# Hybrid attention layer: the rotary chain traced with the second pair of forgetting heads, x's parts added on VectorE, two steps a tile, other banks for the first latent keys

## The chip, the cores and the metric

The kernel runs on one core of one Trainium2 chip. The core has a matrix engine (TensorE, in the profile PE, with its weight loads as PEld), VectorE (DVE), ScalarE (ACT), GpSimd (POOL), SyncE (SP), which here only issues transfers, and 16 DMA engines. On-chip memory is SBUF, and PSUM, eight banks of 128 x 512 numbers into which PE writes. The metric is device time in microseconds, median of the runs shown. Lower is better.

## The reference

The layer takes x (512 tokens, 2048 wide, float32), normalizes it and projects it with one wide matrix. The columns are the latents and gate of eight latent-attention heads (MLA), and queries, keys, values, forget logits and gate of eight forgetting heads (FoX). Both attend causally, both are gated, and one output projection follows.

```python
h = _rms_norm(x, g_pre)
proj = h @ w_in
(q_lat, kv_lat, k_rope_raw, gate_mla,
 fq, fk, fv, f_logit, gate_fox) = jnp.split(proj, split_points, axis=-1)
o_mla = _mla_branch(q_lat, kv_lat, k_rope_raw, g_q, w_uq, g_kv, w_ukv, cos, sin) * jax.nn.silu(gate_mla)
o_fox = _fox_branch(fq, fk, fv, f_logit, b_forget) * jax.nn.silu(gate_fox)
o = jnp.concatenate([o_mla, o_fox], axis=-1) @ w_out
return x + _rms_norm(o, g_post)
```

In the MLA branch the latents are normalized and projected up to queries, keys and values; 64 of the 192 query and key numbers of a head are turned by the rotary tables, the sine and cosine of position times frequency. In the FoX branch the logits get the running sum of the log of a sigmoid of the forget logits (the scan below).

## The kernel before, in words

**Numbers.** Products run at nearly full float32 precision from rounded parts. Each operand is divided into a high part (a copy rounded on ScalarE, line 290 for weights) and a low part (the rest, subtracted on VectorE, line 291), and PE adds three products (lines 152 to 154). A weight tile is 128 x 1024 numbers. `chunk` (line 291 is in its helper `divide`) loads tiles four ahead and divides them two ahead; the pools whi and wlo hold three tiles each.

**Products.** Large projections (values "v" and gate "g" of the forgetting heads, latents and MLA gate, the values' up projection, the output) run as seven block products instead of eight, p1, p2, g5, g3, g7, q6, p4, on sums and differences of blocks. This needs differences of the blocks of x: `x_steps(j)` for j = 0 to 3 puts four pairs of x's high and low parts together again (tile xr, line 1117), then `away_steps` subtracts blocks (tile rmg, line 1016), keeps one difference divided (smg), and sends the others to DRAM through POOL's queue (awaymg, line 1006), to be fetched later on SyncE (bmg, line 1045). Tiles of x parts, copied values and the first scaled query share one pool of four, differences and many weight tiles a pool of 28 slots.

**Stages.** First x is transposed, and a part of the projection (with the forget logits) runs to 42 us. Then come the first forgetting queries (`fox_q(0, ...)`, tile fq), with the forget sums (`forget_sums`: powers, logs, ends, rows, scan) beside it; then p1 of the values (tile va) and of the gate (ga), p2, and the other products. Four pairs of forgetting heads follow (`for p in range(4)`): in round p the queries of pair p are projected while the scores of the pair before run, and the keys while that pair's probabilities meet the values. Then the latent products, four pairs of MLA heads (`mla_q`, `mla_k`, `mla_values`), and the output.

**Order.** Work beside the matmuls stands in a list, `todo`. After each k tile of a product `pump(rate)` takes that many steps off the list and traces them; `wait(n)` puts in n empty steps; `drain()` traces all that is left. The order in which the code traces instructions is their priority. A planner then sets each engine's order, ahead of the run: from the instructions whose inputs it expects to be ready, it takes the one traced first. So an instruction that is ready early may stand far ahead of its place in the code. On the chip each engine, and each of the DMA queues of SyncE and POOL, works in that order, and what waits holds up all behind it. `queued()` ties a load on SyncE behind the weight load traced last. In the first projection the orders of PE, ScalarE and VectorE are as written.

**Rotary tables.** `rotary_tables` (traced after product g3 of the gate) issues five small loads on SyncE (lines 874 and 876: frequencies and positions), then steps: one cast and eight other scalings on VectorE and sixteen steps of subtracting turns or the like (lines 883 to 918, tile angles), three sines on ScalarE (lines 917 to 920), one write to DRAM on POOL (line 921), eight loads on SyncE that spread the tables (line 926). The tables are first used by the rotary key, after the forgetting heads.

**Banks.** PSUM's eight banks are four for projections (`proj_bank`), three for attention (`att_bank`) and one more ("pv"). `mla_q(0)` takes three projection banks, from which small copies (tile mw, line 126) and other work read; the first keys `mla_k(0, ...)` follow a product uA, which has one projection bank and "pv".

Of the kernel before, what the change touches and what calls it, by code (L numbers as in the profile page):

```python
# [65 lines left out]
def tile_hybrid_layer(  # L66
# [36 lines left out]
    def bank(tag, name, bufs):  # L103
        return ps.tile([P, 512], F32, tag=tag, name=name, bufs=bufs)

    def proj_bank(name):
        return bank("pj", name, 4)

    def att_bank(name):
        return bank("at", name, 3)  # L110
# [481 lines left out]
    def wait(n):  # L592
        todo.extend([lambda: None] * n)
# [19 lines left out]
    def proj_T(rng, outs, kh, kl, rate=1, ahead_load=4):  # L613

        k = 0
        n_k = sum(chunks[i][3] for i in rng)
        for i in rng:
            hi, lo = chunk(i, ahead_load)
            for j in range(chunks[i][3]):
                for o, rows, pick in outs:  # L620
                    mm3(o[:rows, :], pick(hi, j), pick(lo, j), kh[k], kl[k], k == 0, k == n_k - 1)
                k += 1
                pump(rate)
                paced(hi)
# [244 lines left out]
    def rotary_tables():  # L869
        ifc = cst.tile([P, 2], F32, name="ifc")  # L870
        rows = cst.tile([P, 3, P], F32, name="angles")
        r, n1, n2 = (rows[:, i, :] for i in range(3))
        with queued():
            nc.sync.dma_start(ifc, inv_freq)
            for b in range(NT):
                nc.sync.dma_start(
                    r[32 * b : 32 * (b + 1), :].bitcast(I32),
                    positions[:, b * P : (b + 1) * P].to_broadcast([32, P]),
                )
        steps = []  # L880

        def angles():
            dve.tensor_copy(n1, r.bitcast(I32))
            dve.tensor_scalar(out=r, in0=n1, scalar1=ifc[:, 0:1], scalar2=None, op0=ALU.mult)

        steps.append(angles)

        def turns(n, c):
            def step():
                dve.tensor_scalar(out=n, in0=r, scalar1=1.0 / c, scalar2=RND, op0=ALU.mult, op1=ALU.add)  # L890
                dve.tensor_scalar(out=n, in0=n, scalar1=-RND, scalar2=None, op0=ALU.add)

            steps.append(step)

        def take(n, parts):
            for c in parts:
                steps.append(
                    lambda c=c: dve.scalar_tensor_tensor(
                        out=r, in0=n, scalar=-c, in1=r, op0=ALU.mult, op1=ALU.add
                    )  # L900
                )

        turns(n1, 2 * math.pi * 4096)
        take(n1, BIG_TURN[:4])
        turns(n2, 2 * math.pi)
        take(n2, TURN[:3])
        take(n1, BIG_TURN[4:])
        take(n2, TURN[3:])
        turns(n1, 2 * math.pi)
        take(n1, TURN[:4])  # L910
        to = dr.tile([P, 3 * P], F32, name="tables")

        def sines():
            lim = 3.1415925
            dve.tensor_scalar(out=r, in0=r, scalar1=lim, scalar2=-lim, op0=ALU.min, op1=ALU.max)

            act.activation(n2, r, AF.Sin, scale=-1.0)
            dve.scalar_tensor_tensor(out=n1, in0=r, scalar=-1.0, in1=r, op0=ALU.mult, op1=ALU.max)
            act.activation(r, r, AF.Sin)
            act.activation(n1, n1, AF.Sin, scale=-1.0, bias=half)  # L920
            pool.dma_start(to, rows.rearrange("p n c -> p (n c)"))

        def spread():
            for g in range(4):
                for table, n in ((sinT, 2 * (g % 2)), (cosT, 1)):
                    nc.sync.dma_start(
                        table[32 * g : 32 * (g + 1), :].rearrange("f (b c) -> f b c", b=NT),
                        to[:, n * P : (n + 1) * P].rearrange("(b f) c -> f b c", b=NT),
                    )

        return [*steps, sines, spread]
# [177 lines left out]
    def x_steps(j):  # L1109

        pair = []

        def whole(h, i):
            if not pair:
                pair.extend(v_block(f"xr{n}{j}") for n in range(2))
            k = 2 * j + 8 * h + i
            pool.tensor_tensor(out=pair[h][:, i, :], in0=hh[k].bitcast(F32), in1=hl[k].bitcast(F32), op=ALU.add)
            if h and i:
                todo.extendleft(reversed(away_steps("m", j, pair, keep="g5")))

        return [lambda h=h, i=i: whole(h, i) for h in range(2) for i in range(2)]
# [1 line left out]

    o_of = []

    def fox_q(p, qb, place):

        proj_T(fox[p]["q"], [(qb[i], P, two[i]) for i in range(2)], hh, hl)
        both = place(f"fqr{p}")
        for i in range(2):  # L1130
            dve.scalar_tensor_tensor(
                out=both[:, i, :], in0=qb[i], scalar=SC_F, in1=rrow, op0=ALU.mult, op1=ALU.mult
            )
        return both

    def fox_q_parts(p, both):

        wholes = slot(f"fw{p}")
        q = []
        for i in range(2):  # L1140
            q.append(split(both[:, i, :], f"fq{p}{i}", first=P))
            whole_block(wholes, i, both[:, i, :])
        return q, wholes
# [92 lines left out]
    def gate_step(h):  # L1236

        g = gate_slots[h // 2][:, h % 2, :]
        gate_of(g, g, f"f{h}")
# [12 lines left out]
    def two_of(make, name):  # L1252
        return [make(f"{name}{i}") for i in range(2)]
# [10 lines left out]
    pool.dma_start(l4_away, l4.rearrange("p t c -> p (t c)"))  # L1264
    dg = diagonals(rcol, "rrow")
    fs = forget_sums(rft)
    wait(2)
    todo.append(lambda: make_row(rrow, "rrow", *dg))
    set_pace(1000)
    todo.extend(fs[:3])  # L1270
    wait(1)
    todo.extend([*x_steps(0), *fs[3:], *x_steps(1)])
    places = [(g, j) for g in "vg" for j in range(4)]
    for g, j in places[:5]:
        fill(prods["p1", g][j], vr.tile([P, 1024], F32, tag="raw", name=f"raw{g}{j}", bufs=5))
    q0 = fox_q(0, [att_bank("fq00"), bank("pv", "fq01", 1)], v_block)
    for g, j in places[5:]:
        fill(prods["p1", g][j], wp.tile([P, 1024], F32, tag="raw", name=f"raw{g}{j}", bufs=3))
    drain()
# [98 lines left out]
    for g in "vg":  # L1378
# [4 lines left out]
    products(  # L1383
        "vg", ("g5", "g3", "g7", "q6", "p4"),
        {
            ("g5", "v"): (1, d3), ("g5", "g"): (1, f7), ("g3", "g", "after"): lambda: todo.extend(rotary_tables()),
            ("g3", "v"): (1, d7), ("g3", "g"): (1, f6), ("g7", "v"): (1, d6),
        },
        out_of,
# [16 lines left out]
    for p in range(4):  # L1406
        if p:
            todo.extend(lambda h=h: gate_step(h) for h in (6 - 2 * p, 7 - 2 * p))
            q, wholes = fox_q_parts(p, fox_q(p, two_of(proj_bank, f"fq{p}"), slot))
            drain()  # L1410
            keys = [load_keys(2 * (3 - p) + i, wholes) for i in range(2)]
            vt = load_v(3 - p, v_slot(3 - p))
            enqueue_values(heads)
            todo.insert(10, split_v(3 - p, vt))
            k = fox_k(p, wholes)
            keys = [forget_keys(*a) for a in keys]
            drain()
        else:
            keys = [forget_keys(*a) for a in keys]
            vt = v_slot(3)  # L1420
            later = split_v(3, vt)
        if p == 2:
            with queued():
                nc.sync.dma_start(gains[0:6, :], g_q.rearrange("o (k p) -> (o k) p", p=P))
                nc.sync.dma_start(gains[6:10, :], g_kv.rearrange("o (k p) -> (o k) p", p=P))
            make_gcol(gains, NK, 10)
        vs = values_of(f"fv{3 - p}")
        heads = []
        for i in range(2):
            h = 2 * (3 - p) + i  # L1430
            heads.append(
                Head(
                    f"f{h}", [q[i]], [k[i]],
                    vs[i],
                    lambda h=h: gate_slots[h // 2][:, h % 2, :],
                    [tuple(wholes[:, 0, c * P : (c + 1) * P] for c in (i, 2 + i))], keys[i],
                )
            )
        enqueue_scores(heads, 1)
        if p == 0:  # L1440
            todo.insert(12, lambda vt=vt: load_v(3, vt))
            todo.append(later)
# [7 lines left out]
    def raw(i):  # L1450
        return raws_of[(i // 2 + 1) % 5][:, i % 2, :]
# [15 lines left out]
    def latent_stats(j):  # L1467
        for s in stats_steps(j):
            s()
# [115 lines left out]
    beside.clear()  # L1585
    room.close()
    todo.extend(lambda i=i: latent(i, raw(i)) for i in range(4))
    todo.append(lambda: latent_stats(0))

    def gate_later(h):  # L1590
# [53 lines left out]

    def mla_k(p, wholes):

        kb = [proj_bank(f"mk{p}{i}") for i in range(2)]
        proj_T(mla[p]["k"], [(kb[i], P, two[i]) for i in range(2)], *k_parts, 2, 6)
        kw = [[whole_block(wholes, 2 + i, kb[i]), krw] for i in range(2)]
        return [[split(kb[i], f"mk{p}{i}"), tuple(keys_turned)] for i in range(2)], kw  # L1650
# [283 lines left out]
```

## Time and profile before

| | us |
|---|---|
| median of 3 runs | 905.74 (904.56 to 906.33) |
| profiled execution | 907.51 |
| its span, first to last instruction | 905.7 |
| PE busy | 879.7 |
| VectorE busy | 633.0 |
| ScalarE busy | 499.9 |
| POOL busy | 145.9 |
| PE's mean granted clock | 0.989 of full speed |

The profile is of one execution. Its page gives busy times, the span in 40 slices and the costliest groups; other views group instructions by tile or line, list who waited for whom, and give busy time by stage. Tiles stand as output<-inputs, without buffer numbers. Matmuls overlap, so that their single durations add up to more than PE's time.

### The profile page before, as it was taken

The page shows a single profiled execution, that of the slowest core. Times are in us where ns is not written, and L with a number is a line of the kernel's source. Part 1 is how long each engine was busy: PE and PEld are TensorE (multiplying, and loading weights), DVE is VectorE, ACT ScalarE, POOL GpSimd, SP SyncE. Part 2 cuts the span into 40 slices and gives each one's busy share as a digit, 9 for nine tenths or more (in the row PEclk, how much of TensorE's full clock was granted, in tenths as well). Part 3 has the DMA queues.
Part 4 walks back from the last instruction along what each step waited for, and adds up shares of the span by engine and source line. Part 5 has one row for each costly group of instructions (what it writes and reads, how often), then busy time and mean ns, then how long its engine had stood idle before and what let it go on. Part 6 is the DMA issues. An engine that isn't in the chain of part 4 may idle for free.

```text
span 905.7 us, 13772 instructions
## 1 busy us (share of the span) xinstructions
PE 879.7 (97%) x5078; PEld 775.1 (86%) x5078; DVE 633.0 (70%) x1043; ACT 499.9 (55%) x914; POOL 145.9 (16%) x148
## 2 busy tenths in 40 slices
PE   8995899999999999999999999999999999999996
PEld 8984799999988888888999999977788888887885
DVE  4669856658555454646677678789787886988786
ACT  6932454435336354544755445547766877646383
POOL 2136402442110100100004442200000000000021
PEclk9997999999999999999999999999999999999999
DMA  9486978999669788794689999985959645799878
GB/s 287 121 282 185 285 229 198 220 229 230 156 147 219 189 228 241 189 264 123 198 294 253 247 223 239 229 217 125 233 141 237 176 132 185 241 321 307 277 216 249
DMA packets 128488, 198.41 MB, mean 219 GB/s; under 512 B 16338, under 2 KB 61292, under 8 KB 127396
## 3 DMA queue, kind: packets, MB, share of 16 engines
q1 hardware_dynamic: 101428, 136.28, 48.2%
q0 software_dynamic: 26256, 61.02, 34.3%
q8 instruction: 40, 0.66, 0.3%
q10 hardware_dynamic: 736, 0.22, 0.1%
q14 instruction: 28, 0.23, 0.1%
HBM read 182.60 MB, written 44.25 MB: 250 GB/s over the span
## 4 chain that ended last, share of the span: by engine, by line
PE 78%; DVE 9%; DMA 6%; ACT 3%; issue 2%; SPq 1%; DVEq 0%; ACTq 0%
PE fk L152 3%; PE fk L154 3%; PE fk L153 3%; DVE wlo L291 3%; PE fq L152 2%; PE fq L154 2%; PE fq L153 2%; PE sm L698 2%; PE in L655 2%; PE sf L698 2%; PE oa L154 2%; PE oa L153 2%; PE oa L152 2%; PE mq L154 1%; PE mq L153 1%
## 5 line engine op out<-in xcount | busy, mean ns | idle before, releaser
L291 DVE TENSOR_TENSOR wlo<-raw,whi 128x1024 fp32r<-128x1024 f32 (+3 forms) x159 | 186.7, 1177 | 108.7 <-ACT whi L290 106.1
L290 ACT CAST whi<-raw 128x1024 fp32r<-128x1024 f32 (+3 forms) x159 | 160.4, 1012 | 142.7 <-PE fk L153 35.5
L152 PE MATMUL fk<-h,whi 128*128 128x512 f32 x128 | 52.5, 410 | 0.0
L152 PE MATMUL fq<-h,whi 128*128 128x512 f32 x128 | 50.9, 397 | 0.0
L154 PE MATMUL fk<-h,wlo 128*128 128x512 f32 x128 | 50.3, 393 | 0.0
L153 PE MATMUL fk<-h,whi 128*128 128x512 f32 x128 | 50.0, 391 | 0.0
L154 PE MATMUL fq<-h,wlo 128*128 128x512 f32 x128 | 50.0, 391 | 0.0
L153 PE MATMUL fq<-h,whi 128*128 128x512 f32 x128 | 49.9, 390 | 0.0
L290 ACT CAST whi<-rawv 128x1024 fp32r<-128x1024 f32 x24 | 25.2, 1049 | 41.1 <-PE gg L153 11.0
L291 DVE TENSOR_TENSOR wlo<-rawl,whi 128x1024 fp32r<-128x1024 f32 x25 | 30.5, 1224 | 22.6 <-ACT whi L290 22.4
L291 DVE TENSOR_TENSOR wlo<-rawv,whi 128x1024 fp32r<-128x1024 f32 x24 | 30.3, 1268 | 22.9 <-ACT whi L290 21.3
L290 ACT CAST whi<-rawl 128x1024 fp32r<-128x1024 f32 x25 | 26.2, 1049 | 35.3 <-PE mc L153 7.9
L290 ACT CAST whi<-rawg 128x1024 fp32r<-128x1024 f32 x24 | 25.2, 1051 | 34.9 <-PE vc L154 8.4
L291 DVE TENSOR_TENSOR wlo<-rawg,whi 128x1024 fp32r<-128x1024 f32 x24 | 29.2, 1222 | 13.7 <-ACT whi L290 13.7
L716 ACT ACTIVATE pf<-pf,stf 128x128 f32<-128x128 f32 (+3 forms) x32 | 18.0, 562 | 30.7 <-DVE stf L707 30.6
L1754 POOL DMA_DIRECT2D c<-in_x_dram x8 | 7.0, 972 | 172.3 <-ACT c L1753 172.2
L243 POOL DMA_DIRECT2D rawl<-in_w_in_dram x20 | 23.8, 1189 | 44.7 <-DVE wlo L291 26.2
L152 PE MATMUL mq<-ln,whi 128*128 128x512 f32 x72 | 29.5, 410 | 0.8 <-ACT whi L290 0.8
L655 PE MATMUL in<-whi,h 128*128 128x328 f32 x128 | 30.0, 321 | 0.0
L153 PE MATMUL mq<-ln,whi 128*128 128x512 f32 x72 | 28.8, 400 | 0.0
L154 PE MATMUL mq<-ln,wlo 128*128 128x512 f32 x72 | 28.7, 401 | 0.0
L154 PEld LDWEIGHTS fk<-h,wlo 128*128 128x128 f32 x128 | 24.0, 188 | 5.4
(625 smaller groups left out, 2948.6 us busy)
## 6 DMA issues: line engine op xcount, KB each, us to landing
raw<-in_w_in_dram SPq DMA_DIRECT2D x62, 512.0 KB
raw<-in_w_out_dram SPq DMA_DIRECT2D x32, 512.0 KB
rawl<-in_w_in_dram POOLq DMA_DIRECT2D x20, 512.0 KB, 10.8
rawv<-in_w_in_dram POOLq DMA_DIRECT2D x16, 512.0 KB, 8.3
rawg<-in_w_in_dram POOLq DMA_DIRECT2D x16, 512.0 KB, 9.8
raw<-in_w_in_dram POOLq DMA_DIRECT2D x12, 512.0 KB, 9.9
bmg<-awaymg SPq DMA_DIRECT2D x20, 256.0 KB
rawl<-in_w_in_dram SPq DMA_DIRECT2D x10, 512.0 KB
```

What stands on the lines that cost most here:

```text
L152: pe.matmul(o, ah, bh, start=first, stop=False, **kw)
L153: pe.matmul(o, ah, bl, start=False, stop=False, **kw)
L154: pe.matmul(o, al, bh, start=False, stop=last, **kw)
L243: pool.dma_start(to, second, accum_op=ALU.add)
L290: act.copy(hi[:, :m], raw[:, :m])
L291: dve.tensor_tensor(out=lo[:, :m], in0=raw[:, :m], in1=hi[:, :m].bitcast(F32), op=ALU.subtract)
L655: pe.matmul(banks[t][:, :n], a[k][:, tss[t]], b[:, j, :], start=k == 0 and m == 0, stop=k == NK - 1 and m == 2,)
L698: pe.matmul(s[:, :nn], a[:, qs], c[:, :nn], start=(i == 0), stop=(i == len(pairs) - 1))
L716: act.activation(p, p, AF.Exp, bias=st[:, 0:1], scale=unit, accum_out=st[:, 1:2])
L1754: pool.dma_start(to, x[piece(t, c)], accum_op=ALU.add)
```

## The change

Six edits. The adds of x's parts go from POOL to VectorE. The first query projection takes two steps off the list after each k tile instead of one. Ahead of the row of scales there are four empty steps instead of two, and an empty step ahead of each of the first three forget steps. The rotary tables are no longer traced after product g3 of the gate, but in round p = 1 of the forgetting heads, after that round's two gate steps and ahead of its query projection. Three empty steps are put ahead of the statistics of the query latents. The first pair's latent keys take attention banks; the other pairs keep projection banks.

```diff
@@ x_steps @@
-            pool.tensor_tensor(out=pair[h][:, i, :], in0=hh[k].bitcast(F32), in1=hl[k].bitcast(F32), op=ALU.add)
+            dve.tensor_tensor(out=pair[h][:, i, :], in0=hh[k].bitcast(F32), in1=hl[k].bitcast(F32), op=ALU.add)
...
-    def fox_q(p, qb, place):
+    def fox_q(p, qb, place, rate=1):
...
-        proj_T(fox[p]["q"], [(qb[i], P, two[i]) for i in range(2)], hh, hl)
+        proj_T(fox[p]["q"], [(qb[i], P, two[i]) for i in range(2)], hh, hl, rate)
...
-    wait(2)
+    wait(4)
     todo.append(lambda: make_row(rrow, "rrow", *dg))
     set_pace(1000)
-    todo.extend(fs[:3])
+    for step in fs[:3]:
+        wait(1)
+        todo.append(step)
     wait(1)
     todo.extend([*x_steps(0), *fs[3:], *x_steps(1)])
...
-    q0 = fox_q(0, [att_bank("fq00"), bank("pv", "fq01", 1)], v_block)
+    q0 = fox_q(0, [att_bank("fq00"), bank("pv", "fq01", 1)], v_block, 2)
...
-            ("g5", "v"): (1, d3), ("g5", "g"): (1, f7), ("g3", "g", "after"): lambda: todo.extend(rotary_tables()),
+            ("g5", "v"): (1, d3), ("g5", "g"): (1, f7),
...
             todo.extend(lambda h=h: gate_step(h) for h in (6 - 2 * p, 7 - 2 * p))
+            if p == 1:
+                todo.extend(rotary_tables())
             q, wholes = fox_q_parts(p, fox_q(p, two_of(proj_bank, f"fq{p}"), slot))
...
     todo.extend(lambda i=i: latent(i, raw(i)) for i in range(4))
+    wait(3)
     todo.append(lambda: latent_stats(0))
...
-        kb = [proj_bank(f"mk{p}{i}") for i in range(2)]
+        kb = [(proj_bank if p else att_bank)(f"mk{p}{i}") for i in range(2)]
```

## The prediction

> **What bounds the kernel now.** I read first the page: busy shares and the 40 slices (each digit tenths of 22.6 us).
>
> ```profile
> PE 879.7 (97%) x5078; PEld 775.1 (86%) x5078; DVE 633.0 (70%) x1043; ACT 499.9 (55%) x914; POOL 145.9 (16%) x148
> ...
> PEclk9997999999999999999999999999999999999999
> ```
>
> TensorE (PE) is the bound, with 97% busy. So an edit is worth only what it gives back where PE waits or runs at a reduced clock. The fourth slice, 68 to 91 us, is the weak one: the clock is 7 tenths. Next, the waits of PE (total, times, longest).
>
> ```profile
> PE va L153 <- DVE wlo L291: 11.5, 2, 9.2
> PE mix L1779 <- ACT scaler L1778: 2.2, 1, 2.2
> PE mk L152 <- ACT mw L126: 1.3, 1, 1.3
> ...
> PE lbq L1480 <- DVE ls L1462: 1.1, 1, 1.1
> ```
>
> The largest wait has one cause: VectorE (DVE) delivers the low parts of two weight tiles of the value product late, by 9.2 and 2.3 us. Then busy time by stage, first across that stretch, and after it the stretches at half clock (columns: us, busy and count of PE, PEld, DVE, ACT, POOL, then clock, DMA share, GB/s):
>
> ```profile
> 42.00:65.00 23.00, 23.00 (x105) 19.03 (x104) 15.72 (x47) 11.07 (x20) 4.15 (x6) 1.00 0.91 300
> 65.00:71.00 6.00, 6.00 (x30) 5.04 (x29) 5.78 (x7) 1.05 (x1) 5.93 (x6) 1.00 0.56 87
> 71.00:81.00 10.00, 0.81 (x4) 0.39 (x3) 9.92 (x12) 2.51 (x3) 5.13 (x5) 0.76 0.36 89
> 81.00:103.00 22.00, 19.72 (x120) 17.76 (x120) 20.91 (x24) 8.85 (x13) 15.37 (x14) 0.88 1.10 280
> ...
> 80.70:86.50 5.80, 5.80 (x14) 4.54 (x15) 5.62 (x8) 1.04 (x1) 4.91 (x4) 0.50 1.05 358
> 103.50:107.00 3.50, 3.50 (x10) 2.74 (x9) 3.43 (x6) 2.10 (x4) 0.57 (x1) 0.51 1.06 320
> 608.70:612.10 3.40, 3.40 (x9) 2.64 (x8) 1.51 (x6) 0.75 (x2) 0.00 (x0) 0.50 0.94 196
> ```
>
> From 65 to 103 us DVE is busy 36.6 of 38 us. Behind each of the two waits PE works at half clock, 5.8 us and 3.5 us, and loses half of each, 2.9 + 1.7 = 4.6 us. The third dip, at 608.7, stands behind the wait of lbq. The timelines of DVE and GpSimd (POOL) show what DVE did instead of the weights (start, duration, what, and in brackets the idle time before it):
>
> ```profile
> 62.80 0.23 DVE L883 CAST angles<-angles 128x128 f32<-128x128 int32 x1 [5.64 <-DMA angles<-in_positions_dram]
> ...
> 78.35 3.42 DVE L291 TENSOR_TENSOR wlo<-rawv,whi 128x1024 fp32r<-128x1024 f32 x2
> 65.75 7.64 POOL L1117 TENSOR_TENSOR xr<-h 128x512 f32<-128x512 f32 x6
> ```
>
> DVE stood 5.64 us before the first rotary step, since the positions had not landed. Then the rotary chain ran beside POOL's adds of x's parts, and the weight PE wanted came only at 78.35. The groups of the rotary tile (ns: min/median/max) with their sum over 42 to 112 us, the x adds on POOL, and the nearest DVE row for such an add (same shape, two SBUF inputs):
>
> ```profile
> L898 DVE SCALAR_TENSOR_TENSOR angles<-angles x15: 291/293/3706, 64.9 to 100.6; 128x128 f32<-128x128 f32 x15
> L890 DVE TENSOR_SCALAR angles<-angles x3: 221/228/1201, 64.4 to 88.2; 128x128 f32<-128x128 f32 x3
> ...
> sum 70.00, DVE 19.59 ACT 0.91 POOL 0.62; mean DVE 3.27 ACT 0.15 POOL 0.10
> L1117 POOL TENSOR_TENSOR xr<-h x16: 1280/1326/2123, 6.6 to 98.2; 128x512 f32<-128x512 f32 x16
> L1016 DVE TENSOR_TENSOR rmg<-xr,xr x4: 673/684/694, 48.3 to 104.2; 128x512 f32<-128x512 f32 x4
> ```
>
> A step of 0.29 us took up to 3.71, one of 0.23 up to 1.20. The late weight has three parents: the wait for positions, the rotary chain, and its slowing beside POOL's adds. The change takes out all three.
>
> **Part 1: rotary chain out, x's adds onto VectorE.** DVE loses 19.6 us of rotary work there (16 steps of 0.29 and 9 of some 0.23, 6.8 us undisturbed; 12.8 was slowing) and the 5.64 us wait. It gains 16 adds x 0.684 = 10.9 us. Its work from 42 to 103 was 15.72 + 5.78 + 9.92 + 20.91 = 52.3 us; now 52.3 - 19.6 + 10.9 = 43.6. PE's work in that stretch without waits and half clock is 61 - 11.5 - 2.9 = 46.6 us. DVE is thus 94% full: enough, without much to spare. A matmul takes 0.22 us (23.00 us for 105), a weight tile 12 of them, 2.6 us; tiles are prepared two ahead, so a weight may be 5.3 us late unnoticed. DVE is one queue: behind each add stand the differences (rmg) and the weights. The adds wait for nothing new, since x's high and low parts are there from the first projection on. SyncE loses 5 + 8 rotary DMAs here, POOL 16 adds and one write.
>
> What is late next, when the value weights are on time, is the next product's weights. Their loads stand on SyncE behind a write that waits for DVE's scan:
>
> ```profile
> SPq L848 <- DVE fz L847: 18.6, 1, 18.6
> ...
> 76.36 0.40 SPq L255 DMA_DIRECT2D raw<-in_w_in_dram  x1
> ```
>
> PE would want them 14 us earlier than it did. Here the two steps a tile matter: the scan is issued within the query projection, not after it, and DVE can run it before 65 us. The empty steps added between the forget steps cost no work; I give them nothing.
>
> Of the 11.5 + 4.6 = 16.1 us, bounds for what stays: 0 if every weight keeps inside its 5.3 us, 16.1 if DVE is no faster. At 94% I expect one wait of the smaller kind that the waits show, 2.3 us, without a dip. **Gain 13.8.**
>
> [...]
>
> **Part 2: the chain with the second pair of forgetting heads.** It is now traced inside the second query projection, its loads queued on SyncE behind the weight loads of that stage. It brings there 25 DVE instructions (6.8 us), three sines and table loads on ScalarE, 5 + 8 DMA issues on SyncE, one on POOL. The stage before, a table load of ScalarE, and two rows of the heads' start:
>
> ```profile
> 262.00:311.00 49.00, 49.00 (x235) 40.59 (x234) 27.27 (x62) 25.50 (x56) 5.31 (x5) 1.00 0.89 207
> ...
> 95.44 1.28 ACT L917 ACT_TABLE_LOAD   x1
> ...
> 263.02 1.29 DVE L142 TENSOR_TENSOR fk<-fkt,fk 128x512 fp32r<-128x512 f32 x2
> 267.56 0.52 PE L698 MATMUL sf<-fk,fq 128*128 128x256 f32 x3
> ```
>
> PE is full for 49 us, DVE has 22 us free, ScalarE 23. The cover is PE's own matmuls. ScalarE pays the sine load as before and one more load back to the exponential, 1.28 us (2 x 1.28 for each time an exponential falls between the sines). The tight place is the start of the heads: the low key part ends at 264.3 and the score matmul that uses it starts at 267.56, 3.3 us of slack. If DVE stands as long as before for positions (5.64) and the chain follows (6.8), 12.4 - 3.3 = 9.1 us are late, and with them the scores, then the banks they hold. Bounds 0 to 9.1; as the chain only fills free places and the DMA is less loaded (207 against 300 GB/s), nearer the low end: **cost 1.0.**
>
> **Part 3: banks of the first latent keys.** Behind the query product PE waits 1.3 us for small copies to free its banks. The row of the key's weight:
>
> ```profile
> 606.59 1.22 DVE L291 TENSOR_TENSOR wlo<-raw,whi 128x1024 fp32r<-128x1024 f32 x1
> ```
>
> It was ready at 607.8, long before, so another free bank lets PE go on: gain 0 to 1.3. A loss would need scores that want the attention banks first, and they need these keys. **Gain 1.3.**
>
> **Part 4: three empty steps before the latent statistics.** PE waits 1.1 us for the last of four adds of squares, between which DVE does other work (the third row: matmuls of the query product before that wait):
>
> ```profile
> 605.39 0.68 DVE L964 TENSOR_TENSOR ruq<-lc,rug 128x512 f32<-128x512 f32 x1
> 605.99 0.68 DVE L1462 TENSOR_TENSOR ls<-ls,lq 128x512 f32<-128x512 f32 x1
> 595.70:606.50 10.80, 9.94 (x43) 7.98 (x43) 0.00 (x0) 0.00 (x0) 1.00 0.88 258
> ```
>
> The statistics ran after 43 of 54 matmuls, in the fifth of six k tiles. Traced after the fourth tile instead of the third they still stand ahead of the place where they ran, so the order can well stay. Bounds: 0, or the wait and its dip, 1.1 + 1.7 = 2.8. I take **0**.
>
> **Sum.** 13.8 - 1.0 + 1.3 + 0 = 14.1 us. The profiled execution took 907.51 us, 905.7 of span and 1.8 around it, and would take 893.4. The median shown, 905.74, is 1.8 lower; against it the forecast is **891.6 us**.
>
> **Rivals.** (a) All of it: no wait stays and part 4 works: 16.1 + 1.3 + 2.8 = 20.2, 885.5. For it: DVE's free room; against: 94%. (b) VectorE remains the bound of the stretch: two waits of 2.3 us, each with a dip of 1.7, stay, 8.0 in all: gain 16.1 - 8.0 + 1.3 - 1.0 = 8.4, 897.3. For it: the x work of one round, four adds, four differences and a split, 9 x 0.68 = 6.1 us, is over the 5.3 us of lead. (c) The wait moves with the chain into the heads: part 2 costs 9.1 and a dip of 1.7: gain 13.8 + 1.3 - 10.8 = 4.3, 901.4. For it the 5.64 us wait; against it the lighter DMA and 22 us of free DVE. (d) The second dip stays though its wait goes, 1.7 less: 893.3; only the order of dip and wait speaks against it. (e) Nothing changes, 905.7: the adds are on VectorE but the weights stay as late, since something else in its queue stands before them. (f) Slower: DVE's differences wait for their tiles, which the transfers to DRAM must free (last column: median us to landing):
>
> ```profile
> awaymg<-rmg POOLq DMA_DIRECT2D x8, 512.0 KB, 6.8
> ```
>
> Adds that come earlier press on the same tiles, and a difference that stands in DVE's queue for a transfer holds the weights behind it. One blocked transfer costs 6.8 us; DVE has 46.6 - 43.6 = 3.0 of room and 5.3 of lead. Above 8.3 us all goes to PE; the 16.1 are used up from 24.4 us on, and with four whole transfers, 27.2, PE loses 18.9 where it lost 16.1: 905.7 + 2.8 - 1.3 + 1.0 = 908.2. Against it: before, no DVE wait named these transfers.
>
> **How the numbers follow.** Forecast (887 to 896) 49%, a 12, b 17, c 8, d 5, e 3, f 6. This measurement can tell about 0.2%, 1.8 us, from no change, so faster means below 903.9: 49 + 12 + 17 + 5 and three quarters of c, 89%; same: e and the rest of c, 5%; slower: f, 6%. The range 884.5 to 901 holds a, the forecast, b, d and the better half of c, and leaves out about 13%.
>
> **What would show it.** Right: PE's wait for DVE's weights in the value product gone or under 3 us; PEclk 9 in the fourth slice; rotary steps at 0.23 and 0.29 us, near the stage that begins at 262 us; x adds on DVE near 0.68 us; the wait for mw gone; the second query and key stage still near 49 us with PE full. Wrong: DVE waiting for positions or for the transfers awaymg; scores waiting on DVE in 262 to 311; a weight wait that remains at 9 us, which would make DVE's amount of work, not the slowing, the cause.

## The result, and the profile after

The changed kernel takes 889.12 us (median, 888.77 to 891.36) against 905.44 of the kernel before beside it (904.56 to 906.33): a ratio of 0.9825, with a 95% interval of 0.9806 to 0.9844. That is 16.3 us; the forecast was 14.1, 891.6 us. The profiled execution took 889.44 us, 18.1 less than the one before. First its page: busy time, and PE's clock in 40 slices.

```profile
PE 874.5 (99%) x5078; PEld 771.3 (87%) x5078; DVE 627.8 (71%) x1059; ACT 505.9 (57%) x919; POOL 125.2 (14%) x132
...
PEclk9999999999999999999999999999999999999999
```

The weak fourth slice is gone: its clock is 9 where it was 7. PE's waits (total, times, longest):

```profile
PE mix L1784 <- ACT scaler L1783: 2.2, 1, 2.2
...
PE rf L840 <- DVE rft L807: 0.9, 1, 0.9
PE mg L154 <- DVE wlo L291: 0.9, 1, 0.9
PE lbq L1484 <- DVE ls L1466: 0.8, 1, 0.8
PE uC L152 <- ACT suq L141: 0.4, 1, 0.4
```

The 11.5 us for the value weights and the 1.3 for mw are gone, and so is one of 0.8 us in the later query products (below). New are 0.9 us for rft (the forgetting rows) and 0.4 and 0.2 us at uC. Busy time in the stretch in which PE had stood (us, then PE, PEld, DVE, ACT, POOL with counts, clock, DMA share, GB/s):

```profile
42.00:65.00 23.00, 22.06 (x101) 18.00 (x100) 18.80 (x47) 11.10 (x20) 5.92 (x8) 1.00 1.02 350
65.00:71.00 6.00, 6.00 (x28) 4.99 (x27) 5.40 (x8) 2.11 (x2) 1.21 (x1) 1.00 1.04 263
71.00:81.00 10.00, 10.00 (x62) 8.95 (x61) 9.93 (x14) 5.80 (x7) 5.51 (x6) 1.00 1.10 271
81.00:103.00 22.00, 22.00 (x143) 20.11 (x142) 12.04 (x13) 10.59 (x13) 4.24 (x6) 1.00 1.02 288
```

From 71 to 81 us, where PE did 0.81 us of work, it does 10.00. From 81 on VectorE is no longer full: 12.04 of 22. The rows of the rotary tile, of x's adds and of the scan (ns min/median/max, first and last start):

```profile
L898 DVE SCALAR_TENSOR_TENSOR angles<-angles x15: 282/292/294, 242.6 to 258.0; 128x128 f32<-128x128 f32 x15
...
L1117 DVE TENSOR_TENSOR xr<-h x16: 681/686/693, 6.8 to 79.9; 128x512 f32<-128x512 f32 x16
...
L847 DVE TENSOR_TENSOR_SCAN fz<-rf,fz x1: 1217/1217/1217, 60.5 to 60.5; 8x512 f32<-8x512 f32 x1
```

No rotary step is slowed any more (294 ns at most, 3706 before). The scan runs at 60.5 us. The first adds start at 6.8 us, in the opening. So I count the adds from 42 to 103 us alone, before and then after:

```profile
L1117 POOL TENSOR_TENSOR xr<-h x12: 1282/1380/2123, 65.7 to 98.2; 128x512 f32<-128x512 f32 x12
```

```profile
L1117 DVE TENSOR_TENSOR xr<-h x8: 683/686/689, 66.2 to 79.9; 128x512 f32<-128x512 f32 x8
```

Of the 16 adds 12 ran in this stretch before, and 8 do now. A whole round of four moved into the opening, and the four differences behind it run between 53 and 59 us, while the queries are projected. This is the work of the pace (two steps a tile and the empty steps between): in every run below with two steps a tile 8 adds fall into the stretch, in every run with one step 12, whichever engine adds. Where the time came from is read from the first starts of the same matmuls, before and then after:

```profile
L152 PE MATMUL vg<-whi,smg x16: 389/389/396, 126.6 to 136.8; 128*128 128x512 f32 x16
...
L152 PE MATMUL mq<-ln,whi x72: 388/395/628, 595.8 to 718.2; 128*128 128x512 f32 x72
...
L152 PE MATMUL uG<-whi,sug x8: 389/391/481, 657.0 to 669.9; 128*128 128x512 f32 x8
...
L1777 PE MATMUL mix<-xr,ident x2: 486/486/486, 896.8 to 897.1; 128*128 128x384 f32 x2
```

```profile
L152 PE MATMUL vg<-whi,smg x16: 389/389/396, 110.9 to 121.1; 128*128 128x512 f32 x16
...
L152 PE MATMUL mq<-ln,whi x72: 387/393/495, 580.5 to 699.9; 128*128 128x512 f32 x72
...
L152 PE MATMUL uG<-whi,sug x8: 389/396/478, 638.6 to 651.5; 128*128 128x512 f32 x8
...
L1782 PE MATMUL mix<-xr,ident x2: 485/486/486, 878.7 to 879.0; 128*128 128x384 f32 x2
```

The value and gate products after the first are 15.7 us earlier. At the latent queries it is 15.3, so the heads with the rotary chain in them cost 0.4 at most (0.3 of it is the wait at mg behind the heads, 0.9 us where it was 0.6). At the latent up product uG it is 18.4, so the end part gave 3.1. At the close it is 18.1.

### The profile page after: what moved, and what is told of

It reads as the page before. It is cut to its first block, busy times and chain, and to the rows that moved or that the text cites. A ratio compares the mean times of both kernels' runs of the same rounds, so it can differ in the third digit from the quotient of the medians.

```text
span 887.7 us, 13764 instructions
## 1 busy us (share of the span) xinstructions
PE 874.5 (99%) x5078; PEld 771.3 (87%) x5078; DVE 627.8 (71%) x1059; ACT 505.9 (57%) x919; POOL 125.2 (14%) x132
## 4 chain that ended last, share of the span: by engine, by line
PE 82%; DVE 8%; DMA 5%; ACT 2%; issue 2%; SPq 1%; DVEq 0%; ACTq 0%
PE fk L154 3%; PE fk L152 3%; PE fk L153 3%; PE in L655 3%; PE fq L152 3%; PE fq L153 3%; PE fq L154 3%; DVE wlo L291 3%; PE sm L698 2%; PE sf L698 2%; PE mq L153 1%; PE mq L154 1%; PE od L153 1%; PE mq L152 1%; PE od L154 1%
## 5 line engine op out<-in xcount | busy, mean ns | idle before, releaser
L291 DVE TENSOR_TENSOR wlo<-rawl,whi 128x1024 fp32r<-128x1024 f32 x25 | 30.5, 1224 | 23.3 <-ACT whi L290 23.1
L154 PEld LDWEIGHTS fq<-h,wlo 128*128 128x128 f32 x128 | 24.0, 188 | 5.4
```

What stands on the lines that cost most here:

```text
L154: pe.matmul(o, al, bh, start=False, stop=last, **kw)
L291: dve.tensor_tensor(out=lo[:, :m], in0=raw[:, :m], in1=hi[:, :m].bitcast(F32), op=ALU.subtract)
```

## The experiments

**Which of the three edits did it?** Adds on VectorE, the chain's new place and the pace act on the same stretch. Three runs take one of them back from the changed kernel, three put one alone into the kernel before, and one loads the positions early there. Each stands against the kernel before, run beside it: 905.01 us for the first four, 906.80 for the next four, 906.50 for the last four.

*Adds back on GpSimd.*

```diff
-            dve.tensor_tensor(out=pair[h][:, i, :], in0=hh[k]...
+            pool.tensor_tensor(out=pair[h][:, i, :], in0=hh[k]...
```

> The changed kernel with one part undone: x's parts are added on GpSimd again; the rotary chain stays in the heads, two steps a tile stay. Theory A (the late weight comes from the chain: its wait for positions, its steps, and their slowing beside GpSimd's adds): without the chain there is nothing to slow, VectorE has 52.3 - 19.6 = 32.7 us of work in the stretch of 46.6, PE's wait for the value weights stays under 3 us, the time is 888 to 893. Rival B (GpSimd's adds are the cause by themselves: they slow any VectorE work beside them, and the differences stand in VectorE's queue for adds of 1.3 us and more): a wait of some us for the weights comes back, VectorE's adds of differences or weight parts last over 1 us, the time is 895 to 903.

Measured: 891.26 us, ratio 0.9847 (0.9819 to 0.9875). PE's wait, and two rows of VectorE's timeline (start, duration, what, idle time before it):

```profile
PE ga L154 <- DVE wlo L291: 1.8, 1, 1.8
```

```profile
69.98 0.69 DVE L1016 TENSOR_TENSOR rmg<-xr,xr 128x512 f32<-128x512 f32 x1 [1.17 <-POOL xr L1117]
...
78.20 6.17 DVE L291 TENSOR_TENSOR wlo<-rawg,whi 128x1024 fp32r<-128x1024 f32 x1 [1.59 <-ACT whi L290]
```

The time is theory A's, but rival B's mechanism is there: a weight's low part of 1.22 us lasted 6.17 beside GpSimd's adds, and a difference stood for an add. Without the chain VectorE had the room to swallow both but for 1.8 us.

*Chain back at its old place.*

```diff
-            ("g5", "v"): (1, d3), ("g5", "g"): (1, f7),
+            ("g5", "v"): (1, d3), ("g5", "g"): (1, f7), ("g3", "g", "after"): lambda: todo.extend(rotary_tables()),
...
-            if p == 1:
-                todo.extend(rotary_tables())
```

> The changed kernel with another part undone: the rotary chain runs again where it ran before, in the stretch of the value products; the adds stay on VectorE, two steps a tile stay. Theory A: VectorE has 43.6 us of work there, 6.8 of undisturbed chain (steps at 0.23 and 0.29 us, since GpSimd is silent) and a stand of 5.6 for positions, 56.0 in all against 46.6 of PE's work and 5.3 of lead: 4.1 us late and a half clock behind that costs 1 to 2, so 893 to 897. Rival B (the adds on GpSimd were the cause, the chain is harmless once they are gone): 888 to 891, no wait for the value weights. Rival C (the stand for positions and the chain's place are all of the cause, whatever the steps last): a wait of 9 us, 900 to 905.

Measured: 889.96 us, ratio 0.9828 (0.9805 to 0.9852). That is rival B's time, and there is no wait for a value weight, only 0.7 at ga. VectorE stood 0.9 us for the positions, since the second round's differences and the scan now ran ahead of the chain. Busy time in the stretch:

```profile
42.00:65.00 23.00, 22.05 (x100) 17.97 (x99) 19.87 (x51) 10.63 (x19) 5.41 (x8) 1.00 1.04 357
65.00:71.00 6.00, 6.00 (x28) 4.95 (x28) 5.79 (x14) 2.11 (x2) 1.33 (x2) 1.00 1.08 325
71.00:81.00 10.00, 10.00 (x64) 9.06 (x63) 10.00 (x15) 5.80 (x7) 5.09 (x6) 1.00 1.07 224
81.00:90.00 9.00, 9.00 (x69) 8.63 (x69) 8.86 (x17) 5.20 (x7) 3.55 (x4) 1.00 1.10 230
90.00:103.00 13.00, 12.27 (x67) 10.55 (x66) 5.86 (x9) 6.17 (x10) 0.78 (x2) 1.00 0.91 301
```

VectorE works 50.4 us (19.87 + 5.79 + 10.00 + 8.86 + 5.86) beside 59.3 of PE, and PE stands only those 0.7 us and the 0.9 at rf. That 50.4 is also what theory A had added up (43.6 + 6.8) is chance: its sum has all 16 adds in the stretch, but only 8 ran there (5.5 us, not 10.9), and as much later work moved in. The yardstick, 46.6 us, failed too: with PE running, 12.7 us more of its matmuls fall into the same stretch, and VectorE's work for them with them.

*One step a tile and the old empty steps.*

```diff
-    wait(4)
+    wait(2)
...
-    for step in fs[:3]:
-        wait(1)
-        todo.append(step)
+    todo.extend(fs[:3])
...
-    q0 = fox_q(0, [att_bank("fq00"), bank("pv", "fq01", 1)], v_block, 2)
+    q0 = fox_q(0, [att_bank("fq00"), bank("pv", "fq01", 1)], v_block)
```

> The changed kernel with the pace undone: one step a tile and the old two empty steps in the first query projection; chain in the heads and adds on VectorE stay. Theory A (SyncE's write of the scan's result holds the next product's weight loads, so the scan must run before 65 us): the scan runs some 5 to 10 us later, the loads behind it too, and PE waits 3 to 8 us for the next product's weights: 892 to 897. Rival B (the pace is worth nothing, tiles are loaded far enough ahead): within 1 us of the changed kernel, 888 to 890.

Measured: 892.38 us, ratio 0.9866 (0.9838 to 0.9894), theory A's lower end. The scan runs at 66.0 instead of 60.5. The waits are 1.6 at va and 1.3 in two at ga, not the 3 to 8 expected for the next product's weights. The two at ga go back to loads on SyncE that landed late (rows of ScalarE and of VectorE for the first of them):

```profile
104.49 1.05 ACT L290 CAST whi<-raw 128x1024 fp32r<-128x1024 f32 x1 [1.67 <-DMA raw<-in_w_in_dram]
```

```profile
105.57 1.22 DVE L291 TENSOR_TENSOR wlo<-raw,whi 128x1024 fp32r<-128x1024 f32 x1 [2.46 <-ACT whi L290]
```

The scan's write, at 67.3, did not hold them: the first load was issued at 93.44, when a low part had freed its tile (93.41), the second at 104.11, when a transfer to DRAM had landed (awaymg, 104.06; SyncE's longest wait of this kind in the run is 10.3 us). The wait at va is VectorE's queue: it was busy without a gap from 64 to 77 us, with 12 adds in the stretch from 42 to 103 us instead of 8.

*Positions loaded early in the kernel before.*

```diff
     rft = forget_parts(vb)
+    chain = rotary_tables()
...
-("g3", "g", "after"): lambda: todo.extend(rotary_tables()),
+("g3", "g", "after"): lambda: todo.extend(chain),
```

> The kernel before with one edit: the loads of positions and frequencies for the rotary chain are issued on SyncE at the end of the opening, some 20 us earlier; the chain runs at its old place, the adds stay on GpSimd. Theory A (three parents of the late weight, the stand for positions is 5.6 of them): the stand goes, the longest wait for a value weight falls from 9.2 to about 4, the half clock behind it to about half, the time falls by 5 to 7 us, to 899 to 901. Rival B (the slowing sets it: VectorE fills the freed time with steps that last up to 3.7 us beside GpSimd's adds): less than 2 us are gained, 903.5 to 905.5. Rival C (the stand alone was the cause): the whole 11.5 us wait and its half clock go, 889 to 893.

Measured: 899.89 us, ratio 0.9939 (0.9919 to 0.9959): theory A's time, not its reading. The chain now ran from 48 to 63 us, with no subtracting step over 0.3 us. Yet PE's longest wait for a weight was still 7.8 us, of 8.9. VectorE stood elsewhere, first for one of GpSimd's adds:

```profile
69.74 1.76 DVE L1016 TENSOR_TENSOR rmg<-xr,xr 128x512 f32<-128x512 f32 x1 [4.12 <-POOL xr L1117]
71.53 2.18 DVE L847 TENSOR_TENSOR_SCAN fz<-rf,fz 8x512 f32<-8x512 f32 x1
```

The scan behind it took 2.18 us beside another add (1.22 in the kernel before). So with neither stand nor slowing of the chain, the adds on GpSimd still make weights late, at one step a tile. They are a parent by themselves, not only the chain's partner.

*The pace alone, in the kernel before* (the edit of the third run, the other way round).

```diff
-    wait(2)
+    wait(4)
...
-    todo.extend(fs[:3])
+    for step in fs[:3]:
+        wait(1)
+        todo.append(step)
...
+    q0 = fox_q(0, [att_bank("fq00"), bank("pv", "fq01", 1)], v_block, 2)
```

> The kernel before with the pace alone: two steps a tile and the empty steps in the first query projection; adds on GpSimd and the rotary chain at its old place stay, banks and statistics as before. The earlier runs leave it open whether each of the three edits (adds, chain, pace) gives a share of its own or any two of them give all. Theory A (all three delays stand in VectorE's one queue, and the tiles prepared ahead swallow some 5 us of them, so that a second edit does the rest): 897 to 902. Rival B (GpSimd's adds are the one cause, VectorE's work only shows it): the pace changes nothing, 903 to 905.5. Rival C (three equal and independent shares of the 14 us): 900 to 901, with the waits for value weights near 7.

Measured: 900.01 us, ratio 0.9931 (0.9907 to 0.9955). Rival B falls. The time lies in both other ranges, so this run does not part them; PE's waits are 3.2 us for value weights and 4.4 at ga. The stand for positions fell to 1.3 us: the first step of the chain starts at 62.3, hardly earlier than before (62.8), but VectorE ran the second round's differences (from 53 to 58 us) and the scan (59.8) ahead of it. Another step took the place, the last of the chain, beside four adds on GpSimd (timelines of VectorE and of GpSimd):

```profile
82.65 6.16 DVE L918 SCALAR_TENSOR_TENSOR angles<-angles 128x128 f32<-128x128 f32 x1
```

```profile
83.21 5.45 POOL L1117 TENSOR_TENSOR xr<-h 128x512 f32<-128x512 f32 x4
```

A step of 0.29 us was held until 88.81, when the fourth add had ended (88.66). Behind it PE stood 4.4 us for a weight at ga.

*The adds alone, in the kernel before* (the edit of the first run, the other way round).

```diff
-            pool.tensor_tensor(out=pair[h][:, i, :], in0=hh[k]...
+            dve.tensor_tensor(out=pair[h][:, i, :], in0=hh[k]...
```

> The kernel before with the adds alone: x's parts are added on VectorE; the rotary chain stays at its old place, one step a tile, banks and statistics as before. Theory A (delays in one queue, some 5 us swallowed): the chain's steps go back to 0.29 us, the stand of 5.6 us for positions stays, one wait of 3 to 6 us for a value weight remains, 895 to 899. Rival B (GpSimd's adds are the one cause): the wait goes but for 2 us, 891 to 894. Rival C (equal shares): 900 to 901.

Measured: 899.04 us, ratio 0.9918 (0.9890 to 0.9946), theory A's upper end. The chain's steps are at 0.29 us, and PE waits once for a value weight, 5.8 us (and 1.4 in three at ga). VectorE's queue:

```profile
64.95 0.23 DVE L883 CAST angles<-angles 128x128 f32<-128x128 int32 x1 [8.65 <-DMA angles<-in_positions_dram]
```

VectorE stood 8.65 us for the positions instead of 5.64. It came to them as long after the start of the queries as before (14.5 us); the positions came later (first step 23.1 us after that start, 20.1 before). Why they did is not shown.

*The chain alone, in the kernel before.*

```diff
-("g3", "g", "after"): lambda: todo.extend(rotary_tables()),
...
+            if p == 1:
+                todo.extend(rotary_tables())
```

> The kernel before with the chain alone: the rotary chain runs with the second pair of forgetting heads; adds on GpSimd, one step a tile, banks and statistics as before. Theory A: the stand for positions and the chain go, but the differences still stand for GpSimd's adds as they did for 4 us where the positions came early; one wait of 3 to 6 us for a value weight remains, 895 to 899. Rival B (GpSimd's adds are the one cause): little is gained, 901 to 905. Rival C (equal shares): 900 to 901. The forecast's reading (the chain and its slowing are the late work, the adds only its partner): 892 to 894.

Measured: 897.98 us, ratio 0.9911 (0.9886 to 0.9937), again theory A; the forecast's reading (892 to 894) falls. PE waits 7.0 us for value weights, 5.8 the longest. VectorE:

```profile
67.93 1.76 DVE L1016 TENSOR_TENSOR rmg<-xr,xr 128x512 f32<-128x512 f32 x1 [2.06 <-POOL xr L1117]
```

A difference stood 2.06 us for an add and then took 1.76 us beside the next ones, where such a step took 0.67 to 0.69 in the kernel before.

What follows from the seven: alone, pace, adds and chain give 6.8, 7.8 and 8.8 us, 23.4 together. All three give 16.4 (the run below without parts 3 and 4). Any two of them, with parts 3 and 4, give 12.6 to 15.1. Equal shares (rival C) would leave one third open in each of the pairs; the pairs leave 1 to 4.5 us, and each edit alone gives more than a third. The delays stand in one queue, and once the weights come inside the two tiles of lead, a further edit has little left to win. And a delay that is taken out can be filled by another, as in the run with the pace alone, where GpSimd held a later step. The pace itself works by this queue: it takes a round of adds out of the stretch and puts differences and scan into the time of the stand.

**Parts 3 and 4.** *The changed kernel with the old banks and without the three empty steps:*

```diff
-        kb = [(proj_bank if p else att_bank)(f"mk{p}{i}") for i in range(2)]
+        kb = [proj_bank(f"mk{p}{i}") for i in range(2)]
...
-    wait(3)
     todo.append(lambda: latent_stats(0))
```

> The changed kernel with the old banks for the first latent keys and without the three empty steps ahead of the latent statistics; adds, chain and pace as in the changed kernel. Theory A (the end part gave 2.8 us, as the starts of the later products read: the mk wait of 1.3 and the half clock behind the statistics' wait): 891.5 to 892.5, the wait for mw back and a half clock behind lbq. Rival (only the banks count, 1.3): 890 to 890.8. Rival (neither counts): 888.5 to 889.5.

Measured: 890.42 us, ratio 0.9827 (0.9805 to 0.9848), the rival that counts 1.3. PE's waits:

```profile
PE lbq L1484 <- DVE ls L1466: 1.4, 1, 1.4
PE mk L152 <- ACT mw L126: 1.3, 1, 1.3
...
PE mq L152 <- ACT whi L290: 0.8, 1, 0.8
```

The wait for mw is back, that of lbq is longer (1.4 for 0.8), and a third is back that the kernel before has in the same words: 0.8 us of a later query product for a weight's high part. But no half clock stands behind lbq (1.00 from 587.50 to 594.33), though its wait is longer than the 1.1 us of before; and the run with the chain back, which keeps both parts, has a half clock there (0.50 from 593.0 to 596.4, behind a wait of 1.2). So the runs do not tie the half clock that the end part lost to these edits.

*The old banks alone* (the first line of that diff).

> The changed kernel with the old banks for the first latent keys alone. By the forecast's price the wait of 1.3 us behind the query product comes back and the time rises by 1.3, to 890.0 to 891. Rival (the wait only moves: TensorE then finds the later copies ready, and the wait of 0.6 that the changed kernel has at the first up product goes): a rise of 0.4 to 0.8. Rival (banks are worth nothing): within 0.3.

Measured: 890.10 us, beside 889.43 (888.37 to 890.11) for the changed kernel run again beside it:

> The changed kernel once more, as the measure for the three kernels beside it, whose edits are worth about 1 us: 888.5 to 890.5 by every theory. The waits in its page are the ones already read, and no half clock before the last 10 us.

The ranges overlap; 0.7 us is not told from nothing. The trace says more: with the old banks, but the empty steps left in, neither the wait for mw nor the 0.8 us comes back. The rows of the small copies that free the banks, without the empty steps and with them (first and last start at the end):

```profile
L126 ACT COPY mw<-mq x8: 248/265/269, 598.7 to 705.6; 128x128 f32<-128x128 f32 x8
```

```profile
L126 ACT COPY mw<-mq x8: 244/265/270, 597.3 to 705.9; 128x128 f32<-128x128 f32 x8
```

With the empty steps the copies come 1.4 us earlier, which by itself covers the wait of 1.3. (PE also came 1.5 us later here, behind a half clock, 0.50 from 592.65 to 596.06. In the changed kernel, at full clock, the copies start at 595.7.) So the empty steps, which had been priced at nothing, take these waits too, and for the first of them the banks are at most a second way. The banks without the steps were not tried.

**What covers the chain in the heads?** The chain's steps tripled, each followed by two that subtract zero:

```diff
-            for c in parts:
+            for c in [d for c in parts for d in (c, 0.0, 0.0)]:
```

> The changed kernel with each subtracting step of the rotary chain followed by two more that subtract zero: 30 further VectorE instructions of 0.29 us, 8.8 us, in the stage of the second query and key projection; results unchanged. Theory A (TensorE's own matmuls cover the chain there, VectorE has some 20 us free): no wait in the stage, the time within 0.5 us of the changed kernel. Rival B (the cover is the 3.3 us ahead of the first score matmul, as the forecast's upper bound has it): 3 to 6 us slower, with scores waiting for VectorE.

Measured: 889.23 us against 889.43: no difference. The row of this stretch in the changed kernel run again, then with the tripled chain:

```profile
240.00:280.00 40.00, 40.00 (x186) 33.02 (x185) 27.96 (x79) 28.76 (x56) 4.75 (x5) 1.00 0.81 193
```

```profile
240.00:280.00 40.00, 40.00 (x187) 33.04 (x186) 37.35 (x111) 23.42 (x50) 4.15 (x4) 1.00 0.83 203
```

VectorE is 93% full for 40 us (37.35), and PE does not stand. Theory A holds.

**An attempt at more.**

```diff
-    wait(3)
+    wait(6)
     todo.append(lambda: latent_stats(0))
...
-    todo.extend([*x_steps(0), *fs[3:], *x_steps(1)])
+    second = x_steps(1)
+    todo.extend([*x_steps(0), *second[:2], *fs[3:], *second[2:]])
```

> An attempt at a better version of the changed kernel: six empty steps ahead of the latent statistics in place of three, and the transposes of the forgetting rows two steps later. By the waits it can take 0.9 (rf) and 0.8 (lbq): 887.3 to 888.5, without these two waits. Rival (the late step only moves the wait: the scan and with it the next product's weights, or the latent operands behind the statistics, come late): 889 to 891, with a new wait at ga or a longer one at uC.

Measured: 887.80 us (887.63 to 888.89), ratio to before 0.9802 (0.9782 to 0.9822). The waits at rf and lbq are gone; behind them one grew and one is new:

```profile
PE uC L152 <- ACT suq L141: 0.8, 1, 0.8
PE sm L698 <- DVE mk L142: 0.4, 1, 0.4
```

It is 1.6 us under the changed kernel beside it, as expected. The ranges overlap at the edge, so it is the best median, not a settled gain.

## Why the prediction was right, point by point

**Part 1, gain 13.8.** Right, a little low. The stretch gave 15.2: the 15.7 at vg, less some 0.5 that PE was early at its start (fq began at 42.2, not 42.7). One remaining wait of 2.3 us was expected; PE kept 0.9 at rf, which is new. The three delays that the change was to take out were VectorE's, as forecast, and the value weights are on time.

The step that failed in it is "DVE is thus 94% full: enough, without much to spare". Its term "16 adds x 0.684 = 10.9 us" was mis-sized: 8 adds fell into the stretch, 5.5 us. Four ran in the opening already before, as the row of the adds (from 6.6 us on) told, and the pace moved four more there. Its yardstick, 46.6 us, was PE's work without waits; as the waits go, later products move in, with PE's work (60.1 us from 42 to 103) and VectorE's (46.2). So the share told nothing: the run with the chain back had 50.4 us of VectorE's work there and no value wait, and 93% did no harm in the heads. The 2.3 us taken off for the 94% thus had no ground: 16.1 less the 0.9 at rf is the 15.2 measured.

The "three parents" were named too narrowly. The stand for positions and the slowing are real: without both 5.1 us are gained. But more than the rotary steps lasted longer beside GpSimd's adds, a weight's low part of 1.22 us for 6.17 too, and differences stood in VectorE's queue for adds (4.12 us). The change was more than enough here: two of its three edits would have brought most of it.

**"What is late next": the scan.** Right that the scan would run before 65 us and that the pace counts: at one step a tile the scan came 5.5 us later and the kernel was 3 us slower. But the step between failed: no wait of PE there goes back to the scan's write. The longest, 1.6 us, is VectorE's queue with four more adds in it, and that the pace moves this round of adds out of the stretch was not foreseen. "The empty steps ... cost no work; I give them nothing" stands for the price of the steps. The new 0.9 at rf belongs to the pace: it is there in the run with the pace alone and gone where the pace is undone.

**Part 2, cost 1.0.** It cost 0.4 at most, as the starts read (15.7 at vg, 15.3 at mq). VectorE did not wait for positions there, and no wait of PE lies between 180 and 300 us. The doubt about the sines came true and was covered: three sines, each between exponentials, brought six table loads. Rows of ScalarE's timeline:

```profile
260.92 1.28 ACT L917 ACT_TABLE_LOAD   x1
...
263.16 1.28 ACT L716 ACT_TABLE_LOAD   x1
...
274.17 1.28 ACT L716 ACT_TABLE_LOAD   x1
```

Six loads of 1.28 are 7.7 us of ScalarE, beside PE's full stage. The 3.3 us ahead of the first score were not the cover; tripling the chain showed that.

**Part 3, gain 1.3, and part 4, 0.** Together they were worth about 1 us in the runs (890.42 against 889.12 and 889.43), near the forecast's 1.3, but not as it was split: part 4, priced at 0, takes the wait for mw by itself and the 0.8 us of the query product too, with 0.6 new at uC, and the banks beside it are not told from nothing. That the sum came out near 1.3 is luck. The order stayed as foreseen, 43 matmuls ahead of the statistics. The 3.1 us that the end part gained in the profiled execution are about 1.3 for mw and 0.8 for the query product, less the 0.6 at uC, and the half clock of 608.7 with its 1.7, which the runs do not tie to the change.

**Rivals.** Nothing spoke for (c), (e) or (f): no wait of VectorE named the positions or awaymg. (a) was nearer in part 1 (16.1 for 15.2) but counted all of part 4's 2.8 in. (b) fell with the 94%. (d) did not occur.

## What to carry to other kernels

When an engine that feeds the bound engine is slowed beside another (here a step of 0.29 us that took 6.16), look at everything that its queue did in the stretch of lateness, not only at what stood nearest ahead of the late instruction. Several edits against one queue need not add up (here 23.4 us one by one, 16.4 together): price each against what the others leave, and expect the second to bring most of the rest. An engine's share in a stretch is no limit by itself (here VectorE was 93% full for 40 us, and PE did not stand); ask what is due by the end of the stretch. Before an instruction's price is multiplied by its count, look when each of them runs: a row's first and last start tell if some lie elsewhere.

## What the runs showed of the hardware

**One step of VectorE lasted as long as a train of GpSimd's adds.** The 0.29 us step of the pace run started at 82.65 and ended with the fourth add, 6.16 us later, although the adds were four instructions of some 1.4 us (5.45 together; starts on GpSimd are rough). It was not always so: in the kernel before, beside six adds from 65.75 on (7.64 together), five rotary steps followed each other, each lasting about as long as one add (1.20 to 1.29 us). What decides it no run here shows. And not all of VectorE's work took longer: in the run with the adds back, the queries' scaling, which reads one operand from PSUM, took its usual 0.69 us (1.37 for two from 65.03) beside the adds (from 65.19).

**Where half clock fell.** In the kernel before PE's clock was 0.50 from 76.23 to 86.47, from 103.54 to 106.95 and from 608.71 to 612.12 us, ahead of the close. These stretches are 10.24, 3.41 and 3.41 us long, and the full clock between them 17.07 and 501.76: 3, 1, 1, 5 and 147 times 3.413. Why the lengths fit so is not shown. Two stretches of 3.41 us in that run, each with the stretch behind it (PE's busy time is the value behind the length):

```profile
605.30:608.71 3.41, 2.31 (x14) 1.76 (x14) 3.34 (x8) 1.69 (x3) 0.00 (x0) 1.00 0.85 213
608.71:612.13 3.42, 3.42 (x10) 2.64 (x8) 1.53 (x6) 0.78 (x2) 0.00 (x0) 0.50 0.95 201
100.13:103.54 3.41, 1.13 (x6) 0.73 (x5) 2.81 (x7) 2.32 (x5) 0.62 (x1) 1.00 1.12 206
103.54:106.96 3.42, 3.42 (x10) 2.66 (x9) 3.35 (x6) 2.06 (x4) 0.57 (x1) 0.50 1.07 322
```

And one of the run with one step a tile, with the stretch behind it:

```profile
72.61:76.02 3.41, 1.77 (x10) 1.41 (x9) 3.41 (x6) 1.05 (x1) 0.99 (x2) 1.00 1.03 212
76.02:79.44 3.42, 3.42 (x21) 2.88 (x21) 3.42 (x5) 1.69 (x3) 2.08 (x2) 1.00 1.05 339
```

Behind 1.13 us of matmuls in the stretch came half clock, behind 1.77 it did not. Of the 2.31 at 605.3 about 0.9 are the statistics' matmuls of one column (eight from 606.82 on, the next matmul at 607.71). The sum does not tell it alone: behind 2.32 us in the run with the chain back (589.6 to 593.0) and 2.10 with the old banks alone (589.24 to 592.65) came half clock, behind 2.22 in the run with the adds back (80.37 to 83.78) and 2.35 without parts 3 and 4 (587.50 to 590.91) it did not. Nor does the length of the wait: half clock stood behind the 1.1 us at lbq in the kernel before, and none behind the 1.4 without parts 3 and 4. What decides it these runs do not show.
